# Layer 0's score products: query low parts as 64-row products of both components, issued ahead of the full products

## The chip, the core and the metric

The kernel runs on one core of a Trainium2 chip. It is one program with one launch. The metric is the device time of one execution in microseconds (us), the median over repeated runs; lower is better.

## The reference

The reference is a two-layer encoder trunk on an input of 1 x 1024 x 1024 in float32. Layer 0 mixes tokens by differential attention, layer 1 by multi-head latent attention; each is followed by a gated MLP with a width-3 causal convolution. Only layer 0's attention is touched here. Cut to what matters:

```python
DA_HEADS = 8; DA_HEAD_DIM = 64; Q_BLOCK = 128; CHUNK = 64

def diff_attention(h, w_qkv, ...):
    q, k, v = split(h @ w_qkv)                 # q, k: (s, 8 heads, 2 components, 64)
    q, k = rotate the first 16 of each 64      # v: (s, 8 heads, 128)
    for each block of 128 queries:
        sc = einsum('bqhcd,bkhcd->bhcqk', qb, k) * 64 ** -0.5      # two components c
        p = masked_softmax(sc, k_chunk <= q_chunk)                 # chunks of 64 tokens
        a = p[:, :, 0] - lam * p[:, :, 1]
        o = einsum('bhqk,bkhe->bqhe', a, v)
    return rms_norm(o) * (1 - lambda_init) @ w_o
```

A score thus contracts over 64 numbers, and there are two sets of scores (components c = 0 and 1) for each head and query block.

## The kernel before, in words

**Precision.** Matrix products run on TensorE in a reduced-precision float type. To keep float32 accuracy, each operand is split into a high part (rounded) and a low part (the remainder), and a product is the sum of high x high, high x low and low x high.

**Layout of q and k in layer 0.** TensorE contracts over up to 128 rows (partitions). A head's two components lie in rows 0 to 63 and 64 to 127. For component c the key tile `k[:, c, :]` holds the key's high part in the component's own 64 rows and its low part in the other 64 rows. The query's high tile `qh[:, c]` holds the same high part in both halves. One 128-row product `qh` x `k` therefore gives q_high x k_high + q_high x k_low; it is called the full product below (line 1367). What is left is q_low x k_high. In the kernel before, each component has a tile `ql[c]` of 128 rows: the query's low part in the component's own rows and zeros in the other rows, written once at the start by four memsets (L324). So the low product (line 1366) is also a 128-row product, in which half of the rows multiply by zero.

**Score calls.** `DaStep.scores(j)` computes the scores of one block i = 2p + j of 128 queries (i = 0 to 7) against its n = 128 (i + 1) keys, in blocks of at most 512 columns. There are 8 heads x 8 blocks = 64 such calls. For i up to 3 (n up to 512) both components share one PSUM tile "S" of 1024 columns, each in its own half; for i from 4 on, each component takes a whole "S" tile. There are two such tiles, and everything that uses `big()` shares them. After the products VectorE masks and takes the row maximum (L1370, L1371, L1375), and ScalarE takes the exponential (L1381), which frees the S tile. `weigh` and `turn` combine and transpose the probabilities (L1394, L248), and `product` multiplies by v.

**What runs around them.** `steps` interleaves the 32 attention steps (8 heads x p = 0 to 3) with "units": `da_unit` projects q, k or v of a head for half of the tokens (24 products, on lines 119, 120 and 121), and rotates and splits the result. In a q unit, ScalarE writes `qh` and GpSimd subtracts to make `ql` (the helper `lo`, L130).

**Order.** The program is written in one sequence; a planner with its own timing model then fixes the order of instructions on each engine. On TensorE an instruction that waits for a PSUM tile holds back all behind it on that engine, but the planner may have put other products ahead of it. So the order of the trace isn't the order of the source. Buffers named s, u and h are fixed SBUF places; `ring` hands out a list of places in turn.

Of the kernel before, what the change touches and what calls it, by code (L numbers as in the profile page):

```python
# [10 lines left out]
F32 = mybir.dt.float32  # L11
F32R = mybir.dt.float32r
# [6 lines left out]
P = 128  # L19
# [21 lines left out]
def blocks(n, step=512):  # L41
    return [(a, min(step, n - a)) for a in range(0, n, step)]
# [14 lines left out]
class Trunk:  # L57
# [249 lines left out]
    def diff_attention(self, o_d, prefetch):  # L307
        nc, a = self.nc, self.a

        H = [[[self.at(f"s{4 * half + 2 * part + g}", [P, 4, 512], F32R) for g in range(2)] for half in range(2)] for part in range(2)]  # L310
        tab = self.at("s12", [P, 2, S])
        self.raw = self.ring(*self.cut("s13"))
        self.w = self.ring("s8", "s9", "s10", "s11")
        R = SimpleNamespace(
            k=self.ring("u0", "u1", "u2"), qh=self.ring("u3", "u4"), v=self.ring("u5", "u6", "u7"),
            P=self.ring("u8", "u9", "u10", "u11", "u12"), pT=self.ring("u13", "u14", "u15"),
            o=self.ring("h2", "h3"), fin=self.ring("h4", "h5", "h6", "h7"),
            rope=self.ring("h8", "h9", "h10", "h11"),
        )

        R.ql = [[self.at(place, [P, 512], F32R) for place in pair] for pair in (("h0", "h1"), ("h12", "h13"))]
        for pair in R.ql:
            for c, other in ((0, slice(64, 128)), (1, slice(0, 64))):
                nc.gpsimd.memset(pair[c][other].bitcast(F32), 0.0)  # L324
        heads = [dict(q=[None, None], k=[None, None], v=[None, None]) for _ in range(DA_HEADS)]
        raws = {}

        def fetch_w(h, which):
            if h < DA_HEADS:
                raws[h, which] = self.fetch(a["da_wqkv"][h, which], D)  # L330

        def split_w(h, which):
            if h < DA_HEADS:
                raw = raws.pop((h, which))
                w = self.w([P, 2, D], F32R)
                self.hi(w[:, 0, :], raw)
                self.lo(w[:, 1, :], raw, w[:, 0, :], nc.gpsimd)
                heads[h]["w", which] = w[:, 0, :], w[:, 1, :]


        def fetch_x(i):
            x = R.P([P, D])
            nc.sync.dma_start(x, a["x"][i * P : (i + 1) * P, :])
            return x

        def token_tile(i, x):
            r = self.rstd(x, self.big(), D)
            nc.vector.scalar_tensor_tensor(x, x, r, g, ALU.mult, ALU.mult)
            s = slice((i % 4) * P, (i % 4 + 1) * P)
            for kg in range(2):  # L350
                self.turn_blocks(x[:, kg * 512 : (kg + 1) * 512], lambda part: H[part][i // 4][kg][:, :, s])

        def unit(h, which, half):
            hd = heads[h]
            return self.da_unit(R, H, hd["w", which], which, half, hd, tab)

        xs = [fetch_x(0)]
        g = self.gain("s11", a["attn_norm_g"][0])
        xs += [fetch_x(1), fetch_x(2)]
        fetch_w(0, 1)  # L360
        xs += [fetch_x(3)]
        fetch_w(0, 0)
        nc.sync.dma_start(tab, a["rope_da"])
        split_w(0, 1)
        for i in range(4):
            token_tile(i, xs[i])
            if i == 1:
                self.load_constants()
        xs += [fetch_x(4), fetch_x(5), fetch_x(6)]
        fetch_w(0, 2)  # L370
        split_w(0, 0)
        self.run([unit(0, 1, 0)])
        split_w(0, 2)
        fetch_w(1, 1)
        self.run([unit(0, 0, 0)])
        for i in range(4, NT):
            if i + 3 < NT:
                xs += [fetch_x(i + 3)]
            token_tile(i, xs[i])
        self.run([unit(0, 2, 0)])  # L380

        def prepare(t):
            h, p = divmod(t, 4)
            if p == 0:
                split_w(h + 1, 1)
                fetch_w(h + 1, 0)
            if p == 1:
                split_w(h + 1, 0)
                fetch_w(h + 1, 2)
            if p == 2:  # L390
                split_w(h + 1, 2)
            if p == 3:
                fetch_w(h + 2, 1)
            if h + 1 == DA_HEADS:
                prefetch()

        def units(t):
            h, p = divmod(t, 4)
            todo = [[(h, 1, 1), (h, 2, 1)], [(h, 0, 1), (h + 1, 1, 0)], [(h + 1, 0, 0)], [(h + 1, 2, 0)]][p]
            return [unit(*u) for u in todo if u[0] < DA_HEADS]  # L400

        self.steps(lambda t: DaStep(self, R, *divmod(t, 4), heads, o_d), units, prepare, 4 * DA_HEADS)

    def da_unit(self, R, H, W, which, half, hd, tab):

        nc = self.nc
        acc = self.bank("u")
        for k in range(KD):
            wh, wl = (w[:, k * P : (k + 1) * P] for w in W)
            rh, rl = (H[part][half][k // 4][:, k % 4, :] for part in range(2))  # L410
            self.mm3(acc, wh, wl, rh, rl, k == 0, k == KD - 1)
            if k == 3:
                yield
        if which == 2:
            v = R.rope([P, 512])
            nc.scalar.copy(v, acc)  # L416
            yield
            hd["v"][half] = x = R.v([P, 2, 512], F32R)
            self.turn_blocks(v, lambda part: x[:, part, :].rearrange("p (k s) -> p k s", s=P))
            return  # L420
        s = slice(half * 512, (half + 1) * 512)
        r = self.rope(R.rope, acc, tab[:, 0, s], tab[:, 1, s], DA_ROT // 2)
        lo, up = slice(0, 64), slice(64, 128)
        if which == 1:

            hd["k"][half] = k = R.k([P, 2, 512], F32R)
            scale = 64 ** -0.5
            for c, own, other in ((0, lo, up), (1, up, lo)):
                nc.scalar.mul(k[own, c, :], r[own], scale)
                nc.vector.scalar_tensor_tensor(k[other, c, :], r[own], scale, k[own, c, :].bitcast(F32), ALU.mult, ALU.subtract)  # L430
        else:

            qh, ql = hd["q"][half] = R.qh([P, 2, 512], F32R), R.ql[half]
            for c, own, other in ((0, lo, up), (1, up, lo)):
                self.hi(qh[own, c], r[own])
                self.hi(qh[other, c], r[own])
                self.lo(ql[c][own], r[own], qh[own, c], nc.gpsimd)

# [904 lines left out]
class DaStep(Step):  # L1345
# [4 lines left out]
    def scores(self, j):  # L1350
        k, nc, hd = self.k, self.k.nc, self.hd
        i = 2 * self.p + j
        n = (i + 1) * P
        qh, ql = hd["q"][i // 4]
        qs = slice((i % 4) * P, (i % 4 + 1) * P)
        nm, l = k.stat(2), k.stat(2)
        one = n <= 512
        sc = []
        for c in range(2):
            if c == 0 or not one:  # L1360
                ps = k.big()
            sc.append(ps[:, c * 512 : c * 512 + n] if one else ps[:, :n])
        for b, m in blocks(n):
            kt = hd["k"][b // 512]
            for c in range(2):
                nc.tensor.matmul(sc[c][:, b : b + m], ql[c][:, qs], kt[:, c, :m], start=True, stop=False)
                nc.tensor.matmul(sc[c][:, b : b + m], qh[:, c, qs], kt[:, c, :m], start=False, stop=True)
        for c in range(2):
            if not one:
                nc.vector.memset(sc[c][0:64, n - 64 : n], NEG)  # L1370
                nc.vector.tensor_reduce(nm[:, c : c + 1], sc[c], axis=AX.X, op=ALU.max, negate=True)  # L1371
        if one:
            both = ps.rearrange("p (c n) -> p c n", c=2)
            nc.vector.memset(both[0:64, :, n - 64 : n], NEG)
            nc.vector.tensor_reduce(nm, both[:, :, :n], axis=AX.X, op=ALU.max, negate=True)  # L1375
        pr = []
        for c in range(2):
            if c == 0 or not one:
                tile = self.R.P([P, S])
            e = tile[:, c * 512 : c * 512 + n] if one else tile[:, :n]  # L1380
            nc.scalar.activation(e, sc[c], AF.Exp, bias=nm[:, c : c + 1], accum_out=l[:, c : c + 1])  # L1381
            pr.append(e)
        self.l.append(l)
        self.probs.append(pr)
# [355 lines left out]
```

## Time and profile before

| what | value |
|---|---|
| time, median of 3 runs (lowest to highest) | 2480.05 us (2479.67 to 2480.57) |
| span of the profiled execution, first to last instruction | 2476.8 us |
| difference of the two | 3.25 us |
| mean granted TensorE clock | 0.992 |
| TensorE matmul busy (PE) | 2376.1 us, 96% |
| TensorE weight loads busy (PEld, beside PE) | 2007.7 us, 81% |
| VectorE (DVE) / ScalarE (ACT) / GpSimd (POOL) busy | 1899.8 / 1301.3 / 651.6 us |
| score products of layer 0 | from 48.1 to about 505 us |

The times of the runs are those of the whole program on the device. The profile is of one execution; its span leaves out what lies before the first and after the last instruction, and 3.25 us is what the median stands above it. In the trace, a matmul's shape is given as rows * columns of the array and then the moving tile; a matmul's recorded length overlaps the next one, so that the distance between two starts is what a product costs in a dense stream.

### The profile page before, as it was taken

What the parts mean: (1) busy time and instruction counts of PE and PEld (TensorE: products, weight loads), DVE (VectorE), ACT (ScalarE), POOL (GpSimd) and SP (SyncE); (2) the same over time, 40 slices, a digit from 0 to 9 for tenths busy, and PEclk for the clock granted to TensorE, in tenths of its full rate; (3) what the DMA queues carried; (4) which work ended last, traced back from release to release, by engine and by line L of the source; (5) the groups of instructions that cost most, each with busy time, mean ns of one, the idle gap of its engine ahead of it and who ended that gap; (6) DMA issues with size and microseconds to landing.
All of it is one profiled execution on the core that took longest, in us unless ns stands there. A gap on an engine that the chain in (4) does not pass through costs nothing.

```text
span 2476.8 us, 32625 instructions
## 1 busy us (share of the span) xinstructions
PE 2376.1 (96%) x11960; PEld 2007.7 (81%) x11960; DVE 1899.8 (77%) x3078; ACT 1301.3 (53%) x2417; POOL 651.6 (26%) x512
## 2 busy tenths in 40 slices
PE   6999999899999999999999999999999999999998
PEld 5788787788888888788888788888888888887886
DVE  6667776846788888899853787777368888888997
ACT  5677777844444444444434777776244444444443
POOL 5545554526000000000131666656350000000001
PEclk9999999899999999999999999999999999999999
DMA  4111111314222222543221211113222222227401
GB/s 154 43 35 43 35 35 44 128 59 132 64 83 83 80 90 80 216 159 104 81 90 52 75 39 35 42 54 119 93 85 94 77 85 84 87 77 280 166 5 77
DMA packets 95104, 214.44 MB, mean 87 GB/s; under 512 B 8640, under 2 KB 33856, under 8 KB 94784
## 3 DMA queue, kind: packets, MB, share of 16 engines
q1 hardware_dynamic: 86048, 185.09, 22.4%
q10 hardware_dynamic: 8896, 27.27, 3.0%
q8 instruction: 94, 1.54, 0.3%
q14 instruction: 66, 0.54, 0.1%
HBM read 159.89 MB, written 52.43 MB: 86 GB/s over the span
## 4 chain that ended last, share of the span: by engine, by line
PE 77%; DVE 8%; ACT 6%; issue 3%; DMA 3%; POOL 2%; SPq 0%; ACTq 0%; POOLq 0%; DVEq 0%
PE S L119 13%; PE S L120 13%; PE S L121 13%; PE b L119 8%; PE b L120 8%; PE b L121 8%; PE u L119 3%; PE u L120 3%; PE u L121 3%; PE b L248 2%; ACT u L1381 1%; PE b L182 1%; PE u L1471 1%; PE u L1470 1%; DVE s L130 1%
## 5 line engine op out<-in xcount | busy, mean ns | idle before, releaser
L163 POOL TENSOR_TENSOR st<-st,mhalf 128x1 f32<-128x1 f32 x56 | 33.8, 605 | 1314.0 <-DVE st L162 1304.9
L127 ACT CAST u<-h 128x512 fp32r<-128x512 f32 (+2 forms) x242 | 146.1, 619 | 279.6 <-DVE h L630 255.7
L119 PE MATMUL S<-s,u 128*128 128x512 f32 (+1 forms) x752 | 285.8, 380 | 5.7 <-DVE u L768 3.9
L121 PE MATMUL S<-s,u 128*128 128x512 f32 (+1 forms) x752 | 284.1, 378 | 0.0
L120 PE MATMUL S<-s,u 128*128 128x512 f32 (+1 forms) x752 | 284.0, 378 | 0.0
L119 PE MATMUL b<-s,u 128*128 128x512 f32 x588 | 231.6, 394 | 0.5
L120 PE MATMUL b<-s,u 128*128 128x512 f32 x588 | 229.5, 390 | 0.0
L121 PE MATMUL b<-s,u 128*128 128x512 f32 x588 | 229.4, 390 | 0.0
L678 DVE SCALAR_TENSOR_TENSOR u<-u,conv,u 128x1023 f32<-128x1023 f32 (+1 forms) x176 | 225.2, 1279 | 1.6 <-ACT u L674 1.6
L149 POOL TENSOR_TENSOR u<-u,st 128x384 f32<-128x384 f32 (+7 forms) x160 | 170.1, 1070 | 152.2 <-DVE st L1456 100.8
L119 PE MATMUL u<-s,s 128*128 128x512 f32 x432 | 174.7, 404 | 14.7 <-ACT h L416 6.7
L130 DVE TENSOR_TENSOR u<-b,u 128x512 fp32r<-128x512 f32 (+1 forms) x256 | 158.7, 632 | 38.2 <-ACT u L127 35.7
L127 ACT CAST s<-u 128x512 fp32r<-128x512 f32 (+3 forms) x196 | 128.6, 693 | 96.5 <-PE u L121 35.4
L121 PE MATMUL u<-s,s 128*128 128x512 f32 x432 | 170.2, 394 | 0.0
L120 PE MATMUL u<-s,s 128*128 128x512 f32 x432 | 169.6, 393 | 0.0
L119 PEld LDWEIGHTS S<-s,u 128*128 128x128 f32 x752 | 141.4, 188 | 34.2 <-issue 4.4
L121 PEld LDWEIGHTS S<-s,u 128*128 128x128 f32 x752 | 141.4, 188 | 26.3
L120 PEld LDWEIGHTS S<-s,u 128*128 128x128 f32 x752 | 141.4, 188 | 25.9
L127 ACT CAST u<-b 128x512 fp32r<-128x512 f32 (+1 forms) x256 | 133.8, 550 | 50.1 <-PE b L248 46.3
L681 ACT ACTIVATE u<-u 128x1024 f32<-128x1024 f32 x44 | 46.7, 1062 | 197.2 <-DVE u L678 197.2
L248 PE MATMUL b<-ident,u 128*128 128x128 f32 x864 | 138.3, 277 | 7.9 <-DVE u L130 5.7
L130 DVE TENSOR_TENSOR u<-h,u 128x512 fp32r<-128x512 f32 x162 | 111.4, 688 | 33.0 <-ACT u L127 31.8
(254 smaller groups left out, 6646.5 us busy)
## 6 DMA issues: line engine op xcount, KB each, us to landing
u<-in_ffn_up SPq DMA_DIRECT2D x88, 512.0 KB, 3.8
g_d<-u ACTq DMA_DIRECT2D x44, 512.0 KB, 2.6
u<-in_ffn_down SPq DMA_DIRECT2D x66, 256.0 KB, 5.3
u<-g_d SPq DMA_DIRECT2D x62, 256.0 KB, 4.4
s<-in_da_wqkv SPq DMA_DIRECT2D x24, 512.0 KB, 3.6
x_d<-u SPq DMA_DIRECT2D x16, 512.0 KB, 2.9
s<-x_d SPq DMA_DIRECT2D x8, 1024.0 KB, 8.9
u<-o_d SPq DMA_DIRECT2D x24, 256.0 KB, 2.8
```

The costliest lines, as they stand in the source:

```text
L119: mm(out, lh, rl, start=first, stop=False, skip_group_check=onto)
L120: mm(out, lh, rh, start=False, stop=False, skip_group_check=onto)
L121: mm(out, ll, rh, start=False, stop=last, skip_group_check=onto)
L127: self.nc.scalar.copy(out, src)
L130: (eng or self.nc.vector).tensor_sub(out, src, hi.bitcast(F32))
L149: self.nc.gpsimd.tensor_mul(x, x, s.to_broadcast(list(x.shape)))
L163: nc.gpsimd.tensor_tensor(r, s, self.mhalf, ALU.pow)
L182: self.nc.tensor.transpose(ps[:, k * P : (k + 1) * P], src[:, k * P : (k + 1) * P], self.ident)
L248: self.nc.tensor.transpose(ps[:, j * P : (j + 1) * P], probs[t][:, k : k + P], self.ident)
L678: nc.vector.scalar_tensor_tensor(t[half][:, back:], u[half][:, : S - back], w, t[half][:, back:], ALU.mult, ALU.add)
L681: nc.scalar.activation(t[0], t[0], AF.Silu)
L1381: nc.scalar.activation(e, sc[c], AF.Exp, bias=nm[:, c : c + 1], accum_out=l[:, c : c + 1])
```

## The change

`R.ql` becomes a ring of two tiles of 128 x 512 (places h0 and h12) in place of two pairs of tiles (h0 and h1, h12 and h13), and the four memsets go. A q unit writes component 0's low part into rows 0 to 63 and component 1's into rows 64 to 127 of one tile. In `scores`, the low product of component c now takes only the component's own 64 rows of `ql` and of the key tile; the low products of both components, for all column blocks, stand in the source ahead of all the full products of the call. The number of matmuls, their columns, and the full products are as before.

```diff
-        R.ql = [[self.at(place, [P, 512], F32R) for place in pair] for pair in (("h0", "h1"), ("h12", "h13"))]
-        for pair in R.ql:
-            for c, other in ((0, slice(64, 128)), (1, slice(0, 64))):
-                nc.gpsimd.memset(pair[c][other].bitcast(F32), 0.0)
+        R.ql = self.ring("h0", "h12")
...
-            qh, ql = hd["q"][half] = R.qh([P, 2, 512], F32R), R.ql[half]
+            qh, ql = hd["q"][half] = R.qh([P, 2, 512], F32R), R.ql([P, 512], F32R)
...
-                self.lo(ql[c][own], r[own], qh[own, c], nc.gpsimd)
+                self.lo(ql[own], r[own], qh[own, c], nc.gpsimd)
...
         for b, m in blocks(n):
             kt = hd["k"][b // 512]
+            for c, rows in ((0, slice(0, 64)), (1, slice(64, 128))):
+                nc.tensor.matmul(sc[c][:, b : b + m], ql[rows, qs], kt[rows, c, :m], start=True, stop=False)
+        for b, m in blocks(n):
+            kt = hd["k"][b // 512]
             for c in range(2):
-                nc.tensor.matmul(sc[c][:, b : b + m], ql[c][:, qs], kt[:, c, :m], start=True, stop=False)
                 nc.tensor.matmul(sc[c][:, b : b + m], qh[:, c, qs], kt[:, c, :m], start=False, stop=True)
```

## The prediction

> **What bounds the kernel now.** I read the page first: its busy times, its slices, its chain.
>
> ```profile
> span 2476.8 us, 32625 instructions
> PE 2376.1 (96%) x11960; PEld 2007.7 (81%) x11960; DVE 1899.8 (77%) x3078; ACT 1301.3 (53%) x2417; POOL 651.6 (26%) x512
> PE   6999999899999999999999999999999999999998
> PE 77%; DVE 8%; ACT 6%; issue 3%; DMA 3%; POOL 2%; SPq 0%; ACTq 0%; POOLq 0%; DVEq 0%
> ```
>
> TensorE is the bound nearly everywhere. The change touches one stage, from about 48 to 505 us. So next come the low products' line (where they lie, how often they waited) and one stretch inside the stage, free of its ends.
>
> ```profile
> L1366 PE MATMUL S<-u,h x192: 220/389/796, 48.4 to 504.9; 128*128 128x512 f32 x96, 128*128 128x128 f32 x32, 128*128 128x256 f32 x32, 128*128 128x384 f32 x32
>   ACT u L1381: 18.0, 13
> core 0: us, PE busy (x) PEld busy (x) DVE busy (x) ACT busy (x) POOL busy (x), PEclk, DMA share, GB/s
> 50.00:450.00 400.00, 384.70 (x2059) 326.40 (x2058) 284.01 (x498) 284.68 (x599) 209.59 (x147) 1.00 0.12 40
> by line: PE u L119 13.5%; PE u L120 12.4%; PE u L121 12.1%; ACT u L1381 6.9%; issue 4.6%; PE b L248 4.2%; PE S L1366 4.0%; PE S L1367 3.8%; DVE u L1394 3.3%; DVE st L1371 3.2%; ACT u L127 3.0%; PE b L120 2.3%; PE b L121 2.3%; DVE h L233 2.2
> ```
>
> There are 192 low products, 96 of them 512 columns wide. PE is busy 384.70 of 400 us at full clock, so its work is what counts. But the last row, the chain between 110 and 450 us by line, gives PE's named lines 13.5 + 12.4 + 12.1 + 4.2 + 4.0 + 3.8 + 2.3 + 2.3 = 54.6%; exponentials, maxima and weighing lie on it too. A microsecond put on PE is therefore worth between 0.55 and 1 us of time; I take 0.8, about the middle.
>
> **What a low product costs now.** The timeline of PE; first column start, second recorded length. Distances between starts are what a product takes from the stream.
>
> ```profile
> 228.25 0.28 PE L1366 MATMUL S<-u,h 128*128 128x256 f32 x1
> 228.37 0.28 PE L1367 MATMUL S<-u,u 128*128 128x256 f32 x1
> ...
> 235.29 0.33 PE L1366 MATMUL S<-u,h 128*128 128x384 f32 x1
> 235.46 0.34 PE L1367 MATMUL S<-u,u 128*128 128x384 f32 x1
> ...
> 245.35 0.40 PE L1366 MATMUL S<-u,h 128*128 128x512 f32 x1
> 245.59 0.39 PE L1367 MATMUL S<-u,u 128*128 128x512 f32 x1
> 245.82 0.40 PE L1366 MATMUL S<-u,h 128*128 128x512 f32 x1
> ...
> 246.76 0.23 PE L1366 MATMUL S<-u,h 128*128 128x128 f32 x1
> 246.82 0.27 PE L1367 MATMUL S<-u,u 128*128 128x128 f32 x1
> ```
>
> 0.12 us at 256 columns, 0.17 at 384, 0.24 at 512, 0.06 at 128. If two 64-row products run at once, the second is free, at the best one of these per pair. All 192 paired would save half of 32 x (0.06 + 0.12 + 0.17) + 96 x 0.24 = 11.2 + 23.0 = 34.2, so 17.1 us. All matmuls of this trace have the form 128*128, so none shows a 64-row product, two at once, or a change from one form to the other.
>
> **Do the pairs meet?** The source puts the two components' low products side by side, but each product needs its own S tile, and the planner orders PE by when it believes the tiles are free. For i up to 3 both components share a tile: the four rows at 245.35 to 245.82 and on (i = 3 of head 3) follow each other, so in 32 of the 64 calls the pair meets. For i from 4 on, each component needs a whole tile of two. Head 3, i = 4, then head 2, i = 4:
>
> ```profile
> 246.29 0.40 PE L1366 MATMUL S<-u,h 128*128 128x512 f32 x1
> ...
> 246.93 0.49 PE L119 MATMUL u<-s,s 128*128 128x512 f32 x1
> 247.26 0.39 PE L120 MATMUL u<-s,s 128*128 128x512 f32 x1
> ...
> 253.46 0.39 PE L1366 MATMUL S<-u,h 128*128 128x512 f32 x1
> 254.09 0.45 PE L1366 MATMUL S<-u,h 128*128 128x512 f32 x1
> ...
> 191.19 0.39 PE L248 MATMUL b<-ident,u 128*128 128x128 f32 x2
> 191.33 0.48 PE L1366 MATMUL S<-u,h 128*128 128x512 f32 x1
> 191.65 0.40 PE L1367 MATMUL S<-u,u 128*128 128x512 f32 x1
> 191.88 0.22 PE L1366 MATMUL S<-u,h 128*128 128x128 f32 x1
> 191.94 0.27 PE L1367 MATMUL S<-u,u 128*128 128x128 f32 x1
> 192.05 0.45 PE L1366 MATMUL S<-u,h 128*128 128x512 f32 x1
> ```
>
> In head 3 component 0 goes at 246.29 and component 1 at 253.46, over 7 us later, with projection products between. In head 2 they are close, but component 0's second block (191.88) was put ahead of component 1's first (192.05), though the source has them the other way: component 1's tile was not free when component 0's first block was done. No call with i from 4 on has the two first blocks adjacent; the nearest have three transposes between. Writing the low products ahead makes component 1's tile no earlier, so in these 32 calls I expect low, low, full, full of one component, then the same of the other: 64-row products one after another on the same 64 rows, each as long as now.
>
> **The terms.** 1. *Pairs that meet*: 32 calls, one pair each, 8 per width: 8 x (0.06 + 0.12 + 0.17 + 0.24) = 4.7 us saved at the best. At the worst nothing: each product still needs its own weights, and the 128-column full product at 246.82 shows 0.11 to the next start (246.93) where its columns need 0.06, so short products already go at the pace of weight loads. I take the middle, -2.4 us.
>
> 2. *Changes of form*: a call with i up to 3 goes into the 64-row form and out again, 2 x 32 = 64; with i from 4 on each component does so, 2 x 64 = 128; together 192. Their price is not in the trace, so bounds. Nearest below: the change from a transpose to a product. Two transposes start at 191.19, the 512-column product at 191.33, the next at 191.65; of these 0.46 us a 512-column product takes 0.225 (below), which leaves 0.12 for each transpose, the pace of a short product (0.11 at 246.82). Nothing visible is paid, and the low end is 0. From above: an array that ran empty and starts again:
>
> ```profile
> 229.74 0.50 PE L119 MATMUL u<-s,s 128*128 128x512 f32 x1 [0.85 <-ACT h L416]
> 230.08 0.39 PE L120 MATMUL u<-s,s 128*128 128x512 f32 x1
> 230.30 0.39 PE L121 MATMUL u<-s,s 128*128 128x512 f32 x1
> 230.53 0.39 PE L119 MATMUL u<-s,s 128*128 128x512 f32 x1
> ...
> 229.74 0.19 PEld L119 LDWEIGHTS u<-s,s 128*128 128x128 f32 x1 [1.06 <-ACT h L416]
> 229.85 0.19 PEld L120 LDWEIGHTS u<-s,s 128*128 128x128 f32 x1
> ```
>
> The first product after the stall takes 0.34 to the next start, later ones (230.08 to 230.53) 0.225: 0.115 for weights that could not be loaded ahead. (The same shows with no stall at 246.93: 0.33 behind a short product.) If the array must also run out first, the tail of the product before is added: 0.39 long, 0.225 to the next start, so 0.165. Both together are 0.28, the upper end: 192 x 0.28 = 53.8 us. A change of form is nearest to the restart row, since the array's partition into row groups must hold for all that is in it; whether weights, tail or both are exposed is open, so I take the mean of the two single prices, 0.14: 192 x 0.14 = +26.9 us.
>
> On this the Trainium skill speaks against the change: "TensorEngine Tiling (Array Packing)", Key Properties, says that going from one tiling mode to another, unlike going between tiles, drains the engine. "TensorE: Matmul & The Clock Gate", Single matmul latency, puts the drain at about 175 ns whatever the contraction, which as an estimate would be 192 x 0.175 = 33.6 us. The tail of 0.165 us in the rows above is near that figure, but no row here shows that a change of form pays it.
>
> 3. *S tile waits*: the low products' waits for L1381, 18.0 us in 13 times, are for the tile. Where each component goes by itself, its first product needs the tile as before; in shared-tile calls too. 0. A slower PE finds tiles free sooner, which is part of why I take 0.8 and not 1.
>
> 4. *Four memsets and the query's low part*: POOL loses four memsets at the start.
>
> ```profile
> L324 POOL MEMSET h<- x4: 517/518/519, 1.1 to 3.0; 64x512 f32 x4
> 5.91 0.56 POOL L163 TENSOR_TENSOR st<-st,mhalf 128x1 f32<-128x1 f32 x1 [2.35 <-DVE st L162]
> ```
>
> POOL then idles 2.35 us for VectorE, which hides them: 0. If that wait went, it would be 4 x 0.518 = 2.1 us at most. The subtractions that make `ql` keep number and size, on the same queue; a ring of two tiles is as deep as two pairs. 0. No DMA is moved, and no queue of SP is touched.
>
> **Sum.** -2.4 + 26.9 = +24.5 us on PE, times 0.8 = +19.6. The profiled span would go from 2476.8 to 2496.4, and the median, 3.25 above the span, from 2480.05 to about 2499.
>
> **Rivals.**
> A. *The change of form is free*, like that between transpose and product. Then only term 1 is left: 0 to -4.7, times 0.8, -2 us in the middle: 2478. For it: the row at 191.33. Against: transposes use all 128 rows, as products do. In this case the change does not do what it says, because half of the calls never place a pair together.
>
> B. *Pairs meet everywhere and changes of form are cheap*; this one ends on the other side. If the planner, given the new order, holds component 0's first block until both tiles are free, the whole 17.1 us is on offer at 2 x 64 = 128 changes. It breaks even at 17.1 / 128 = 0.134 us per change and is faster by over 5 us only if (17.1 - 128 x c) x 0.8 > 5, c below 0.085. At c = 0.02: -11.6, 2468. For it: heads 2, 4 and 6, where the components stand within 0.7 us. Against: not one of 32 calls has them adjacent. The tiling page of the Trainium skill, Theoretical Speedup, gives up to a factor of 2 for contractions of 64 or less, which is this case's best.
>
> C. *Each change pays both tail and weights*, 0.28: 53.8 - 2.4 = 51.4, times 0.8 = +41: 2521. For it: a stall shows both in the rows at 229.74. Against: weight loads overlap products everywhere else in this trace.
>
> **How the numbers follow.** Forecast (2489 to 2509) 0.43; A 0.25; B 0.12; C 0.20. A measurement of this kernel tells about 0.2%, 5 us, from no change. Faster by more than that: B, 0.12. Within: A, 0.25. Slower: forecast and C, 0.63. The range reaches down past A (2475 with all of term 1) halfway into B, 2472, and up to C with a little over, 2525; the likeliest case alone has 2489 (0.07 a change) to 2509 (0.2).
>
> **What the profile would show.** Low products in the form 64*128, 192 of them, and the four memsets gone from POOL. Term 1: for i up to 3, two low products starting far closer than 0.24 us apart. Order: for i from 4 on, a component's two low products together and the other component's elsewhere. Term 2: the start distance from the last 128-row product into a 64-row one and back, over 0.225 at 512 columns by 0.14. The stage's end (last score product at 505 us now) moved later by about 20 us, and nothing moved behind it. The prediction is wrong if those distances have no excess, or if the planner's new order brings components together, or if its new order costs or saves time elsewhere in the stage.

## The result, and the profile after

The changed kernel takes 2496.99 us (median of 4 runs, 2494.48 to 2498.85) against 2480.31 us before (median of 4, 2479.67 to 2484.03): a ratio of 1.0066, 95% interval 1.0052 to 1.0081. It is slower by 16.7 us; the interval is 13 to 20 us. The profiled span went from 2476.8 to 2495.4 us, by 18.6.

First the page of the changed kernel: span, busy times, slices of PE, chain by engine.

```profile
span 2495.4 us, 32612 instructions
PE 2403.8 (96%) x11960; PEld 1998.0 (80%) x11960; DVE 1892.0 (76%) x3078; ACT 1302.9 (52%) x2417; POOL 649.2 (26%) x508
PE   7999999999999999999999999999999999999998
PE 83%; DVE 7%; ACT 4%; issue 2%; DMA 2%; POOL 1%; SPq 0%; ACTq 0%; POOLq 0%; DVEq 0%
```

The four memsets are gone from POOL (512 to 508 instructions), all else is as many as before. PE is busy 27.7 us longer with the same 11960 products. Then the same stretch of layer 0 as in the prediction, the chain by line inside it, and the low products' new line.

```profile
50.00:450.00 400.00, 391.92 (x1973) 305.67 (x1972) 265.63 (x484) 274.08 (x577) 201.54 (x142) 1.00 0.11 37
by line: PE u L119 19.1%; PE u L120 18.1%; PE u L121 17.9%; PE S L1367 10.1%; PE S L1363 9.0%; PE b L248 6.0%; PE b L120 3.2%; PE b L121 3.2%; PE b L119 2.9%; ACT u L1381 1.8%; issue 1.6%; DVE st L1371 1.1%; PE b L182 1.0%; PE b L1422 0.7%;
L1363 PE MATMUL S<-u,h x192: 217/426/792, 48.4 to 523.5; 64*128 64x512 f32 x96, 64*128 64x128 f32 x32, 64*128 64x256 f32 x32, 64*128 64x384 f32 x32
```

In 400 us PE gets through 1973 products where it got through 2059, while busier (391.92 against 384.70 us). The score lines' share of the chain rises from 4.0 + 3.8% to 9.0 + 10.1%, and the exponentials' falls from 6.9 to 1.8%: TensorE now waits less for others and is itself slower. The last low product starts at 523.5 instead of 504.9. The timeline of PE shows where (i = 3 of head 3, then i = 4, component 0; "x2" is two products, and the length is from the first's start to the second's end).

```profile
252.39 0.39 PE L121 MATMUL u<-s,s 128*128 128x512 f32 x1
252.72 0.49 PE L1363 MATMUL S<-u,h 64*128 64x512 f32 x2
253.14 0.73 PE L1367 MATMUL S<-u,u 128*128 128x512 f32 x2
253.80 0.56 PE L1363 MATMUL S<-u,h 64*128 64x512 f32 x2
254.29 0.56 PE L1367 MATMUL S<-u,u 128*128 128x512 f32 x2
254.68 0.44 PE L119 MATMUL u<-s,s 128*128 128x512 f32 x1
```

Three things are to be seen. *The pair runs at once:* two low products of 512 columns take 0.49 us together, the length of one; in the trace their starts are 0.003 us apart. *Each change of form costs:* from the product at 252.39 to the low pair 0.33 us pass instead of 0.227, and the first product in a new form is recorded 0.49 or 0.50 us long instead of 0.39, with its successor late by as much. From the product at 252.39 to the next score call at 253.80 it is 1.41 us; before, the same call took 0.94 from 245.35 to 246.29 and the product ahead of it 0.23, 1.17 us in all. The pair saved 0.24 and the call still lost 0.24. (Up to 253.80 the stretch holds two changes and the wait ahead of a third.) *The order is as feared:* at 253.80 come the two low products of component 0's two blocks, then its two full ones, then projection products; component 1 follows more than 7 us later, at 261.29.

Two sums over PE help below. I added the distances between starts of PE's products from the first to the last score product and took out the idle time that the profile gives. This is PE's work in the stage: 433.7 us before, 462.7 after, so +29.0, while idle time fell from 23.3 to 13.3. The stage grew by 19.0. Over that stretch the form changes 194 times and 36 pairs run at once.

A little of the 29.0 is not the form. PEclk, the third number from the end of these rows, is the mean clock that TensorE was granted in a stretch. Between 50 and 550 us it is under 1.00 only here, before and then after:

```profile
450.00:500.00 50.00, 41.98 (x215) 35.33 (x214) 42.16 (x67) 40.15 (x85) 21.48 (x16) 0.86 0.38 133
```

```profile
400.00:450.00 50.00, 48.09 (x244) 37.79 (x244) 33.83 (x64) 34.67 (x75) 24.65 (x18) 0.97 0.16 54
450.00:500.00 50.00, 46.21 (x232) 35.55 (x230) 40.71 (x62) 39.54 (x79) 25.35 (x18) 0.94 0.40 137
500.00:550.00 50.00, 47.80 (x232) 38.18 (x231) 29.84 (x46) 28.25 (x57) 12.86 (x10) 0.92 0.20 64
```

The trace has stretches at full clock and at half, nothing between: 13.7 us at half in this stage before, 17.1 after. At half, a product of 512 columns takes 0.43 us (before, from 479.59 to 480.02). I estimate from this that about 2 of the 29.0 us are due to the clock. Why it was lowered for longer is not shown.

As a landmark behind layer 0 I use layer 1's exponentials; their row gives the start of the first and of the last. Before, then after:

```profile
L1450 ACT ACTIVATE u<-S,st x128: 362/741/1126, 1373.0 to 1718.8; 128x384 f32<-128x384 f32 x16, 128x512 f32<-128x512 f32 x16, 128x128 f32<-128x128 f32 x16, 128x256 f32<-128x256 f32 x16
```

```profile
L1450 ACT ACTIVATE u<-S,st x128: 359/739/1125, 1391.0 to 1737.8; 128x384 f32<-128x384 f32 x16, 128x512 f32<-128x512 f32 x16, 128x128 f32<-128x128 f32 x16, 128x256 f32<-128x256 f32 x16
```

Layer 1 starts 18.0 us later and takes as long as before (345.8 and 346.8 us). The loss lies in layer 0 alone.

### The profile page after: what moved, and what is told of

The parts are those of the page before. It is cut to its first block, busy times and chain, and to the rows that moved or that the text cites. A ratio compares the mean times of both kernels' runs of the same rounds, so it can differ in the third digit from the quotient of the medians.

```text
span 2495.4 us, 32612 instructions
## 1 busy us (share of the span) xinstructions
PE 2403.8 (96%) x11960; PEld 1998.0 (80%) x11960; DVE 1892.0 (76%) x3078; ACT 1302.9 (52%) x2417; POOL 649.2 (26%) x508
## 4 chain that ended last, share of the span: by engine, by line
PE 83%; DVE 7%; ACT 4%; issue 2%; DMA 2%; POOL 1%; SPq 0%; ACTq 0%; POOLq 0%; DVEq 0%
PE S L119 13%; PE S L120 13%; PE S L121 13%; PE b L119 8%; PE b L120 8%; PE b L121 8%; PE u L119 4%; PE u L120 4%; PE u L121 4%; PE b L248 3%; PE S L1367 2%; PE S L1363 2%; DVE s L130 1%; PE b L182 1%; PE u L1471 1%
## 5 line engine op out<-in xcount | busy, mean ns | idle before, releaser
L248 PE MATMUL b<-ident,u 128*128 128x128 f32 x864 | 139.0, 278 | 9.0 <-DVE u L130 5.9
```

The costliest lines, as they stand in the source:

```text
L248: self.nc.tensor.transpose(ps[:, j * P : (j + 1) * P], probs[t][:, k : k + P], self.ident)
```

## The experiments

My theory was that the changes of form cost the time. The rivals were that the planner's new order costs it, and that the pairs would pay if more of them met.

### The new order with 128-row products

```diff
         for b, m in blocks(n):
             kt = hd["k"][b // 512]
             for c in range(2):
                 nc.tensor.matmul(sc[c][:, b : b + m], ql[c][:, qs], kt[:, c, :m], start=True, stop=False)
+        for b, m in blocks(n):
+            kt = hd["k"][b // 512]
+            for c in range(2):
                 nc.tensor.matmul(sc[c][:, b : b + m], qh[:, c, qs], kt[:, c, :m], start=False, stop=True)
```

> The changed kernel's source order (all low products of a call, then all full ones), but with the low products of the kernel before: 128 rows, the other component's rows zero. Form theory (the time is lost where TensorE goes from 128-row to 64-row products and back, about 0.15 to 0.2 us each, 194 times): no such change is left, so the time is that of before, 2475 to 2485. Order theory (the planner's new order costs the time, by S tiles or by what comes between the products): about 2497, as the changed kernel.

Measured: 2466.71 us, ratio 0.9946 (0.9934 to 0.9959). It is faster than before by 14 us, which neither theory had. TensorE goes into low products or out of them 194 times, as in the changed kernel, but in one form. Its products in layer 0 also stand in the changed kernel's order, one by one, except for two neighbours near the start and the last 50 or so of the stage, so that little but the form differs. Its low products and layer 1's exponentials:

```profile
L1366 PE MATMUL S<-u,h x192: 220/389/793, 47.6 to 504.1; 128*128 128x512 f32 x96, 128*128 128x128 f32 x32, 128*128 128x256 f32 x32, 128*128 128x384 f32 x32
L1453 ACT ACTIVATE u<-S,st x128: 352/746/1118, 1372.6 to 1703.7; 128x384 f32<-128x384 f32 x16, 128x512 f32<-128x512 f32 x16, 128x128 f32<-128x128 f32 x16, 128x256 f32<-128x256 f32 x16
```

Layer 0 ends as before (last low product 504.1 against 504.9), and layer 1 starts as before (1372.6 against 1373.0): the order theory falls, the form theory stands. The gain lies in layer 1, whose exponentials span 331.1 us instead of 345.8. No line of layer 1 was edited.

### 64-row products in the order of before

```diff
-                nc.tensor.matmul(sc[c][:, b : b + m], ql[c][:, qs], kt[:, c, :m], start=True, stop=False)
+                nc.tensor.matmul(sc[c][:, b : b + m], ql[rows, qs], kt[rows, c, :m], start=True, stop=False)
                 nc.tensor.matmul(sc[c][:, b : b + m], qh[:, c, qs], kt[:, c, :m], start=False, stop=True)
```

(with the changed kernel's ring and writes of `ql`).

> 64-row low products in the source order of before: low and full of one component, then low and full of the other. No two low products are neighbours, so none can run side by side, and the form changes 384 times. Form theory: twice the changes and no pair, 384 x 0.146 to 0.196 = 56 to 75 us on TensorE, of which two thirds to all show: 2517 to 2555. Order theory: the order is that of before, so about 2480. If only the missing pairs mattered: 2497 plus some 4 us.

Measured: 2535.83 us, ratio 1.0225 (1.0211 to 1.0239). The form changes 384 times, and PE's work in the stage is 506.9 us: (506.9 - 433.7) / 384 = 0.19 us each. Up to the last 50 or so of the stage, TensorE's products stand in the order of before, one by one. But the stage has 23.9 us at half clock, 10.2 more than before, which by the same estimate are some 5 us; without them the mean is 0.18 us. The timeline shows the price bare, at full clock:

```profile
272.63 0.50 PE L1363 MATMUL S<-u,h 64*128 64x512 f32 x1
273.06 0.49 PE L1364 MATMUL S<-u,u 128*128 128x512 f32 x1
273.48 0.50 PE L1363 MATMUL S<-u,h 64*128 64x512 f32 x1
273.91 0.50 PE L1364 MATMUL S<-u,u 128*128 128x512 f32 x1
274.34 0.33 PE L1363 MATMUL S<-u,h 64*128 64x128 f32 x1
274.60 0.33 PE L1364 MATMUL S<-u,u 128*128 128x128 f32 x1
```

The weight loads of the third and the fourth of these products start when the product itself starts (in the prediction's rows one starts at 229.85, ahead of its product at 230.08):

```profile
272.63 0.18 PEld L1363 LDWEIGHTS S<-u,h 64*128 64x128 f32 x1 [0.25 <-issue]
273.05 0.19 PEld L1364 LDWEIGHTS S<-u,u 128*128 128x128 f32 x1 [0.24 <-issue]
```

Starts are 0.43 us apart where 0.235 was the distance before, and 0.26 at 128 columns where it was 0.06: 0.19 to 0.20 at either width, in both directions. Half of it, 0.10 to 0.11, is the longer record (0.50 against 0.39, 0.33 against 0.22), as behind the stall in the prediction's rows, where the weights were not there; 0.09 passes before that start. The profile models the ends of products, so it doesn't show how far the array had run out by then.

### The two halves

The form in calls with i up to 3 alone, and in calls with i from 4 on alone; the other calls keep padded tiles, and all low products are written ahead. The core of the first edit to the changed kernel (the second has 1 for 0):

```diff
-                nc.tensor.matmul(sc[c][:, b : b + m], ql[rows, qs], kt[rows, c, :m], start=True, stop=False)
+                if i // 4 == 0:
+                    nc.tensor.matmul(sc[c][:, b : b + m], ql[rows, qs], kt[rows, c, :m], start=True, stop=False)
+                else:
+                    nc.tensor.matmul(sc[c][:, b : b + m], ql[c][:, qs], kt[:, c, :m], start=True, stop=False)
```

> The changed kernel's form only in calls with i up to 3 (both components in one S tile); calls with i from 4 on keep 128-row low products with zeros, all low products still written ahead. 64 changes of form and 32 pairs side by side. Form theory with 0.18 us a change, as the runs so far gave it: 64 x 0.18 - 4.7 = +7 us on TensorE in layer 0, the stage 4 to 7 us longer than before. Its layer 1 has the planner's order that the kernel with 128-row products in the new source order had, some 14 us shorter: 2470 to 2475 in all. If the price lay in the calls of i up to 3, the stage would be nearer to +19.

> The other half: 64-row low products only in calls with i from 4 on, 128-row ones with zeros for i up to 3. 130 changes of form, few pairs. Form theory: 130 x 0.18 - 1 = +22 us on TensorE, the stage 13 to 18 us longer than before; layer 1 in the planner's longer order, as before and as the changed kernel: 2493 to 2499 in all. With the calls of i up to 3 alone (+4 to 7) the stages' excesses should add up to the changed kernel's 19.

Measured: 2471.0 us (ratio 0.9963, 0.9951 to 0.9976) and 2492.97 us (1.0049, 1.0036 to 1.0063). The first lies in its forecast, the second 0.03 us below its own. Layer 1's exponentials, the first half's and the second's:

```profile
L1456 ACT ACTIVATE u<-S,st x128: 358/744/1120, 1378.1 to 1709.1; 128x384 f32<-128x384 f32 x16, 128x512 f32<-128x512 f32 x16, 128x128 f32<-128x128 f32 x16, 128x256 f32<-128x256 f32 x16
```

```profile
L1456 ACT ACTIVATE u<-S,st x128: 358/740/1127, 1387.5 to 1733.0; 128x384 f32<-128x384 f32 x16, 128x512 f32<-128x512 f32 x16, 128x128 f32<-128x128 f32 x16, 128x256 f32<-128x256 f32 x16
```

Layer 1 starts 5.1 and 14.5 us later than before, 19.6 together, against the changed kernel's 18.0; the first half has the shorter layer 1 (331.0 us), the second the longer (345.5). PE's work rises by 8.3 us (66 changes, 30 pairs) and 20.8 (128 changes, 6 pairs). Even where nearly every pair meets, the form loses: a pair of 512 columns saves 0.24, its two changes cost 0.38. Two neighbours aside, TensorE's products stand in the same order throughout the program in the first half and in the kernel of the new order with 128-row products, and likewise in the second half and the changed kernel. So the form in calls with i up to 3 costs 2471.0 - 2466.71 = 4.3 us by the one comparison and 2496.99 - 2492.97 = 4.0 us by the other, whichever order layer 1 has.

### Both low products on the same rows

```diff
-            for c, rows in ((0, slice(0, 64)), (1, slice(64, 128))):
+            for c, rows in ((0, slice(0, 64)), (1, slice(0, 64))):
```

> The changed kernel, but component 1's low product reads rows 0 to 63 as component 0's does (its low term is then taken from other rows, so the low correction of component 1 is not the reference's). Same number of changes of form, same instructions, but the two components' low products use the same row group and cannot run at once. Theory that the 36 meeting pairs run at once and save their 5.5 us of TensorE time: the start distance inside a pair goes from 0.003 us to over 0.2, and the time rises by 3 to 6 us, 2500 to 2503. Rival, that pairs next to a change of form save nothing because both weight loads are exposed anyway: 2495 to 2498.

Measured: 2490.27 us, ratio 1.0040 (1.0028 to 1.0053). The time missed both forecasts, since this kernel too has the shorter layer 1 (and 190 changes of form, not 194). The distances answer the question (i = 3 of head 3):

```profile
251.52 0.73 PE L1363 MATMUL S<-u,h 64*128 64x512 f32 x2
252.18 0.73 PE L1367 MATMUL S<-u,u 128*128 128x512 f32 x2
```

From the first low product to the first full one it is 0.66 us, against 0.42 in the changed kernel: there the pair does run at once, and saves 0.24. The 36 pairs save 8 x 0.06 + 10 x 0.12 + 7 x 0.17 + 11 x 0.24 = 5.5 us by their widths. Layer 1 starts at 1395.7, 4.7 us later than in the changed kernel. But the planner's order of layer 0 differs too, so I don't give these 4.7 to the pairs alone.

### Pairs made to meet

The call's products keep the written order on TensorE, component 1's low products first:

```diff
+        with k.tc.manual_schedule(engines={mybir.EngineType.PE}):
...
-            for c, rows in ((0, slice(0, 64)), (1, slice(64, 128))):
+                for c, rows in ((1, slice(64, 128)), (0, slice(0, 64))):
```

> The changed kernel with the products of a score call kept in the written order on TensorE, component 1's low products ahead of component 0's; for i from 4 on a call's products then mostly stand in one piece, once both S tiles are free. Changes of form fall from 194 to 172 and most calls' pairs meet. Theory: TensorE saves 22 x 0.2 = 4 us of changes and some 9 us by pairs against the changed kernel, two thirds of it in time, so 2486 to 2492 if holding one S tile for the other costs nothing, and above the changed kernel's 2497 if it does. In no case faster than before: 172 x 0.2 = 34 us of changes against at most 17.1 us saved.

Measured: 2487.51 us, ratio 1.0030 (1.0019 to 1.0042). 71 pairs run at once and the form changes 172 times. The time is what I expected, for a reason that I didn't: layer 1 is again the shorter one, and starts at 1396.0, 5 us later than in the changed kernel. TensorE's work in the stage falls by some 5 us against the changed kernel, where I expected 13; 3.9 us of the difference are 20 other products that now fall into the stage, which ends later. Low and full products of one call, and PE's longest waits in layer 0:

```profile
145.70 0.62 PE L1364 MATMUL S<-u,h 64*128 64x512 f32 x4
146.25 0.96 PE L1368 MATMUL S<-u,u 128*128 128x512 f32 x4
```

```profile
PE S L1364 <- ACT u L1382: 9.4, 9, 3.0
PE b L248 <- DVE u L130: 5.7, 1, 5.7
PE S L1364 <- POOL h L130: 3.8, 3, 1.6
```

Four low products (two pairs, 512 and 256 columns) start and are through in 0.55 us; the second pair pays no price. But idle time in the stage is 25.1 us, 11.8 more than in the changed kernel. Of the rows above, the first is the low products' wait for an S tile (6.4 us in the changed kernel), and the third their wait for the query's low part; the 5.7 us are one wait of the transposes for VectorE. So only a part of the 11.8 is shown to come from holding one S tile for the other. Rival B thus names a real saving, and in this kernel the pairs meet at the price of more waiting.

### The other order of layer 1

The planner's order of layer 1 comes in two kinds in these kernels, and small edits in layer 0 pick one. The kernel before with one head's loop turned round, and the changed kernel likewise:

```diff
-            for c in range(2):
+            for c in range(2)[:: -1 if self.h == 7 else 1]:
```

```diff
-            for c, rows in ((0, slice(0, 64)), (1, slice(64, 128))):
+            for c, rows in ((0, slice(0, 64)), (1, slice(64, 128)))[:: -1 if self.h == 0 else 1]:
```

> The kernel before, 128-row low products and the source order of before, but in layer 0's last head the loop over components runs from 1 to 0. Nothing else differs; the planner's order of layer 1's attention becomes the one of the three kernels that were some 14 us shorter there. If that order is what those 14 us are: layer 0's stage as before, layer 1's attention 394 us and not 408, 2464 to 2470 in all. If they came from layer 0's form or order: 2480.

> The changed kernel, but in layer 0's first head component 1's low products are written ahead of component 0's. Number and form of all products as in the changed kernel; the planner's order of layer 1's attention becomes the shorter one. If layer 0's cost and layer 1's order simply add: layer 0's stage some 19 us longer than before, layer 1's attention 14 us shorter, 2480 to 2486 in all, that is no more than 0.3% from before. If the 14 us need 128-row products in layer 0: 2497.

Measured: 2466.57 us (ratio 0.9946, 0.9934 to 0.9959) and 2488.06 us (1.0032, 1.0020 to 1.0045). Layer 1's exponentials in the one and the other:

```profile
L1450 ACT ACTIVATE u<-S,st x128: 362/746/1120, 1374.8 to 1705.9; 128x384 f32<-128x384 f32 x16, 128x512 f32<-128x512 f32 x16, 128x128 f32<-128x128 f32 x16, 128x256 f32<-128x256 f32 x16
```

```profile
L1450 ACT ACTIVATE u<-S,st x128: 362/744/1119, 1394.8 to 1725.7; 128x384 f32<-128x384 f32 x16, 128x512 f32<-128x512 f32 x16, 128x128 f32<-128x128 f32 x16, 128x256 f32<-128x256 f32 x16
```

Both span 331 us. From layer 1's first exponential on, TensorE's products stand in one and the same order in all six kernels with 331 us, and in another in the four with 346 (but for some 40 products at its start, where the kernel before differs from the other three). So the 14 us go with layer 1's order and not with layer 0's form, and with the shorter order on both sides the changed form still costs 2488.06 - 2466.57 = 21.5 us. (This is more than 16.7: with head 0 turned, layer 1 starts at 1394.8 and not at 1391.0. Its layer 0 has 23.9 us at half clock, 6.8 more than the changed kernel's, which I estimate at 2 to 3 of these 3.8 us.) In the chain from 1400 to 1700 us, before and with head 7 turned, the shorter order has larger shares of TensorE's transposes (L248) and smaller ones of maxima (L1449) and exponentials (L1450):

```profile
by line: PE b L248 10.8%; PE S L119 7.7%; PE u L1471 7.7%; PE S L121 7.6%; PE S L120 7.5%; PE b L119 7.4%; PE u L1470 7.2%; PE b L121 7.2%; PE b L120 7.2%; DVE st L1449 5.8%; issue 5.1%; ACT u L1450 3.4%; DVE u L130 2.4%; DVE s L130 2.1%; A
```

```profile
by line: PE b L248 16.5%; PE u L1471 10.2%; PE u L1470 9.4%; PE S L121 9.2%; PE S L120 9.2%; PE S L119 9.1%; PE b L119 8.3%; PE b L120 7.6%; PE b L121 7.6%; DVE st L1449 2.7%; issue 2.5%; DVE u L130 2.1%; ACT u L1450 1.8%; ACT u L127 1.6%; 
```

Why the planner takes the one or the other stays open. Of all kernels run, the two with 128-row products and this order are the fastest, 2466.6 and 2466.7 us, 0.54% below before; they are there by the planner's choice, not by a design.

## Why the prediction was right, point by point

The forecast of about 2499 us met 2496.99, in the case that it called likeliest: the changes of form cost more than the pairs save. Its parts were not all of the right size, and that their errors cancel is luck.

- **Do the pairs meet?** Right in the main: the new order leaves the two components of most calls with i from 4 on apart. 192 changes and 32 pairs were forecast; 194 and 36 came, 30 pairs in calls with i up to 3 and 6 in the others.
- **The price of a change** (term 2) was too small, 0.14 against 0.19 us. The step that failed is the mean of the two single prices, taken as if either the weights or the tail were exposed. Part of both is paid: the weight load in full (0.10 to 0.11 us, the restart row's 0.115), and 0.09 of waiting ahead of it, about half of the 0.165 tail. This holds at 128 and at 512 columns, so it does not grow with the product's width. The prediction's reason, that the array's row groups must hold for all that is in it, no run shows. "TensorEngine Tiling (Array Packing)" in the Trainium skill, Key Properties, has a change of mode drain the engine; a price is there, 0.19 us, but no row shows when the array was empty. The estimate from "TensorE: Matmul & The Clock Gate" in the Trainium skill, Single matmul latency, 0.175 us, comes close to the whole price; if a drain has to end before the weights load, it is twice the wait seen.
- **The pairs** (term 1): -2.4 was taken from 0 to -4.7. By their widths they saved 5.5: a pair's two weight loads don't spoil it (0.24 saved at 512 columns, by the kernel with both on the same rows), and four pairs more met.
- **The sum on PE** was +24.5 and measured +29.0. With the two sizes above, 194 x 0.19 - 5.5 = 31.4, while the 29.0 are about 27 without the clock. So over the stage a change costs less than in a dense stream, (27 + 5.5) / 194 = 0.17 us. One reason lies in the prediction's rows: at 246.93, behind a 128-column product, 0.10 for the weights was lost before as well, and at least 45 of the changes go from a 128-column to a 512-column product. How much of the 4 us this is I have not separated.
- **What of it is time**: 0.8 was taken and 19.0 / 29.0 = 0.66 came; 0.65 and 0.66 in the two halves and 0.80 at 384 changes. PE's idle time gives way first (23.3 to 13.3 us) and seems to have less to give as the dose grows. This error and that in the price cancel: 24.5 x 0.8 and 29.0 x 0.66 differ by half a microsecond.
- **S tile waits, memsets, GpSimd**: 0 each, as forecast: the low products' waits for the tile are 14.1 us in 14 times (18.0 in 13 before), the first low product starts at 48.4 with and without the memsets, and nothing moved behind the stage.
- **Rivals**: A falls with the rows at 252.39 and the kernel in the new order with 128-row products; C, both prices in full, with the 0.19; B because its pairs don't meet and a change costs more than its break-even of 0.134; the kernel whose pairs were made to meet is slower than before too.
- **Missing**: a rival for the order of layer 1. The prediction's last sentence looked for a new order only inside the stage. Had this edit tipped the planner, as four of the experiments did without being meant to, the time would have been 2483 (14 us less) to 2488 (as measured with head 0's loop turned), with every step of the working unchanged.

## What to carry to other kernels

Running two half-height products at once pays only if the stay in that form is long. In this kernel two changes cost 0.38 us, more than the 0.24 that a pair of the widest products saves, so count the changes in the order that really runs, not in the source. Price a form in a dense stream by the distances between starts; the lengths of records overlap. Where a planner orders the program, compare the stages that were not edited, and the clock that each was granted, before a difference of half a percent is given to an edit: a turned loop in one head of layer 0 made layer 1 14 us shorter.

## What the runs showed of the hardware

Two 64-row products on different row groups start 0.003 us apart and end within 0.013 us of each other (the changed kernel's 36 pairs), here in the reduced-precision float32 type. In a dense stream at full clock, going from the 128-row form to the 64-row one or back costs 0.19 to 0.20 us at 128 as at 512 columns, of which 0.10 to 0.11 is a weight load that is not hidden; over the whole stage the mean is 0.17 to 0.18; inside the form, the next product's weights are hidden again (four low products through in 0.55 us).
